# Mixture-of-experts stage: six more experts in fp32, another order of experts, and an earlier read of the first expert's slots

## The chip, the cores and the metric

One core of a Trainium2 chip runs the whole layer as one launch. The metric is the device time of one execution in microseconds (us); lower is better. TensorE is called PE in the profile, VectorE DVE, ScalarE ACT, GpSimd POOL, SyncE SP. PE's weight loads are listed apart as PEld.

## What is computed

The layer is an attention mixer (neighbourhood attention and grouped-query attention over 1024 tokens and a context of 256) followed by a mixture of 32 experts, of which each token takes 4. The change touches the experts alone. Cut to what matters:

```python
logits = h @ w_router + b_router
top_logits, top_e = lax.top_k(logits, 4)
top_w = softmax(top_logits)
# for each expert e, the tokens xe that chose it:
gu = xe @ w_gu[e] + b_gu[e]                  # 1024 -> 2048
x_glu = minimum(gu[:, :1024], 7.0)
x_lin = clip(gu[:, 1024:], -7.0, 7.0)
act = (x_lin + 1) * (x_glu * sigmoid(1.702 * x_glu))
yb = act @ w_dn[e] + b_dn[e]                 # 1024 -> 1024
y[token] += yb * top_w                       # summed over the 4 experts of a token
x = x + gt2 * rmsnorm(y, g_post_ffn)
```

All data is fp32, and the result must be close to fp32.

## The kernel before

The program runs its phases one after another: modulation and projections, attention, output projections with the router, then the experts (`Moe2.moe`, line 1441), a loop for tokens over the capacities (`overflow`, which has no rounds here), and the last norm (`final`, line 1411).

**Ranks and capacities.** The router's code counts the tokens of each expert and ranks the experts by count. Rank r has room for `CAPS[r]` tokens (line 2056): ranks 0 to 15 for 304 down to 136, ranks 16 to 24 for 128, ranks 25 to 31 for 96 down to 56. The program is fixed for the ranks; which expert has a rank is read from `erow` into a register (`ereg`), and the weight DMAs use it as an address. For each of its ranks the table of slots in DRAM (`slots_d`) lists token number and weight; the router's code writes it by indirect DMAs of POOL, and the last of these end just before the experts begin.

**Three forms of an expert** (`mode`, line 1466). A weight piece is 128 x 1024 fp32 (512 KB); a step works on four pieces, and an expert has six steps: four U steps (of `w_gu`) and two D steps (of `w_dn`), 24 pieces.
- "T", over 128 tokens: the weights are stationary. Each piece is split into two parts, hi (ACT, `split_hi`, line 1523) and lo (DVE, `split_lo`, line 1532), which PE takes in its faster reduced fp32 form; the tokens are split in the same way and stand beside each other, so that a matmul of hi goes over 2c columns and one of lo over 256 (`tra`, lines 1692 to 1697).
- "N", 128 tokens: split as well, with the tokens stationary and 512 columns of weights moving, three matmuls for each (`nat`, lines 1659 to 1668).
- "F", up to 96 tokens: plain fp32, no split. The weights are stationary in halves of 64 columns, two halves side by side (`few`, line 1717). In the trace each of these matmuls shows as two rows, 128 rows a step.

**Order of steps.** `positions()` gives each place p = 0 to 31 a rank: even places take the wide experts from rank 0 (304 tokens) on, odd places first the seven F experts from rank 31 (56) on, then the nine N experts. `steps` (line 1480) weaves the pair p, p + 1: U of p + 1 and U or D of p in turn, with the next pair's first two U steps in between the D steps. In the very last pair no next pair is there, so its two D steps of p + 1 stand behind each other; in the very first, the two U steps of place 0 do.

**Buffers and queues.** SP issues all weight DMAs. Split pieces go to `raw5` (6 buffers), and from there to `hi5` (6) and `lo5` (5); F pieces go to `rawf` (4 buffers, one step). A piece of F is loaded into the buffer that a matmul step has just left (`load_whole`, line 1720, in the second pass of `few`). When the last F expert is done, the space of `rawf` becomes two more buffers each of `hi5` and `lo5`. Splits and loads for the split experts are issued from `slot` (line 1592), called after each piece of a T or N step. `slot` also moves the chains of work behind a step (activation, next split) and takes one item off the queues `hot` and `cold`: transposes of an N expert's activations, of the next expert's gathered tokens (`xtr`), and of results (`one` in `step_D`, line 1861). A call from an F step moves the chains only and leaves these queues alone.

**Results.** `scatter` (line 1879) adds a tile of results to the sums in DRAM (`f_d`) by an indirect DMA of POOL, each behind the one before, as they write the same tensor. `final` reads `f_d` when all have landed.

**Start.** Before, SP loads six pieces of place 0 (line 1903), ACT and DVE split four, and the slots of places 0 and 1 are read from ACT's queue behind the third split (line 1915); `gather(0)` then fetches the tokens and `prepare(0)` transposes them.

## Time and profile before

| | us |
|---|---|
| median of 3 runs | 2760.55 |
| lowest, highest | 2759.66, 2763.95 |
| the profiled execution | 2763.18 |
| its span in the profile | 2761.6 |
| PE busy in the span | 2627.6 (95%) |
| DVE, ACT, POOL busy | 1754.1, 1419.0, 560.7 |

The span is the time from the first to the last instruction of the profiled execution. Its experts run from some 1150 us (first weights asked for) to some 2727 us (sums read). A row of the timeline gives the start, the duration, engine and line, what is written and read, and in brackets how long the engine had been idle and what released it. Matmuls overlap, so the time from one start to the next is what one costs. SPq, ACTq stand for the queue's part: the issue of DMAs.

### The profile page before, as it was taken

The page shows a single profiled execution, that of the slowest core. Times are in us where ns is not written, and L with a number is a line of the kernel's source. Part 1 is how long each engine was busy: PE and PEld are TensorE (multiplying, and loading weights), DVE is VectorE, ACT ScalarE, POOL GpSimd, SP SyncE. Part 2 cuts the span into 40 slices and gives each one's busy share as a digit, 9 for nine tenths or more (in the row PEclk, how much of TensorE's full clock was granted, in tenths as well). Part 3 has the DMA queues.
Part 4 walks back from the last instruction along what each step waited for, and adds up shares of the span by engine and source line. Part 5 has one row for each costly group of instructions (what it writes and reads, how often), then busy time and mean ns, then how long its engine had stood idle before and what let it go on. Part 6 is the DMA issues. An engine that isn't in the chain of part 4 may idle for free. (4 is left out here: it accounts for less than half of the span.)

```text
span 2761.6 us, 52451 instructions
## 1 busy us (share of the span) xinstructions
PE 2627.6 (95%) x19986; PEld 2246.1 (81%) x19986; DVE 1754.1 (64%) x3001; ACT 1419.0 (51%) x2334; POOL 560.7 (20%) x485
## 2 busy tenths in 40 slices
PE   6999999999999999599999999999999999999993
PEld 3788887555588778499999999999999999899892
DVE  3722332667688546554555655566888888888895
ACT  3422111555577424434444445446777777777773
POOL 2310001556644232400110011001101100111001
PEclk9999999999999999799999999999999999999996
DMA  6224561501233243566788898888889988998896
GB/s 240 73 95 162 196 197 60 171 16 33 43 76 74 106 145 132 167 225 222 276 287 272 291 298 287 287 294 286 278 281 309 301 286 299 314 309 293 299 312 227
DMA packets 197423, 588.16 MB, mean 213 GB/s; under 512 B 50400, under 2 KB 57136, under 8 KB 197024
## 3 DMA queue, kind: packets, MB, share of 16 engines
q1 hardware_dynamic: 174432, 521.51, 55.1%
q0 software_dynamic: 19152, 61.86, 8.4%
q8 instruction: 158, 2.59, 0.4%
q10 hardware_dynamic: 3584, 1.40, 0.3%
q14 instruction: 97, 0.79, 0.1%
HBM read 527.92 MB, written 58.08 MB: 212 GB/s over the span
## 5 line engine op out<-in xcount | busy, mean ns | idle before, releaser
L1532 DVE TENSOR_TENSOR lo<-raw,hi 128x1024 fp32r<-128x1024 f32 x600 | 719.5, 1222 | 347.8 <-ACT hi L1523 219.0
L1523 ACT ACTIVATE hi<-raw 128x1024 fp32r<-128x1024 f32 x600 | 626.4, 1054 | 130.5 <-PE g L1692 59.7
L1692 PE MATMUL g<-xT,hi 128*128 128x320 f32 (+10 forms) x1792 | 522.1, 333 | 0.0
L1693 PE MATMUL g<-xT,lo 128*128 128x256 f32 x1792 | 484.2, 281 | 0.0
L1692 PEld LDWEIGHTS g<-xT,hi 128*128 128x128 f32 x1792 | 337.2, 188 | 12.3 <-issue 0.3
L1693 PEld LDWEIGHTS g<-xT,lo 128*128 128x128 f32 x1792 | 337.6, 188 | 1.5
L1881 POOL DMA_INDIRECT f_d<-y,slot x34 | 62.5, 1838 | 1206.0 <-ACT y L1869 1062.7
L1692 PE MATMUL g<-aT,hi 128*128 128x288 f32 (+10 forms) x896 | 262.9, 335 | 0.0
L1693 PE MATMUL g<-aT,lo 128*128 128x256 f32 x896 | 241.8, 280 | 0.0
L174 DVE TENSOR_TENSOR wlo<-raw,whi 128x1024 fp32r<-128x1024 f32 x33 | 42.1, 1290 | 218.5 <-ACT whi L173 218.3
L1692 PEld LDWEIGHTS g<-aT,hi 128*128 128x128 f32 x896 | 168.5, 188 | 5.8
L1693 PEld LDWEIGHTS g<-aT,lo 128*128 128x128 f32 x896 | 168.9, 188 | 0.4
L859 ACT ACTIVATE p<-S 128x512 f32<-128x512 f32 x160 | 94.2, 596 | 103.7 <-PE S L858 99.0
L613 DVE TENSOR_REDUCE mn<-S 128x1 f32<-128x512 f32 x180 | 100.9, 595 | 66.4 <-PE S L612 66.0
L1717 PE MATMUL g<-xN,rawf 128*64 128x88 f32 (+5 forms) x3584 | 131.5, 234 | 1.8 <-issue 0.8
L1717 PEld LDWEIGHTS g<-xN,rawf 128*64 128x64 f32 x3584 | 125.9, 137 | 7.7 <-issue 5.6
L400 PE MATMUL mm<-hTh,whi 128*128 128x512 f32 (+1 forms) x416 | 123.9, 385 | 1.7 <-ACT whi L173 1.7
L400 PE MATMUL mm<-hTh,wlo 128*128 128x512 f32 (+1 forms) x416 | 123.2, 384 | 0.0
L400 PE MATMUL mm<-hTl,whi 128*128 128x512 f32 (+1 forms) x416 | 123.1, 383 | 0.0
L1666 PE MATMUL g<-hi,xN 128*128 128x512 f32 x288 | 117.6, 408 | 0.0
L1668 PE MATMUL g<-lo,xN 128*128 128x512 f32 x288 | 113.7, 395 | 0.0
L1667 PE MATMUL g<-hi,xN 128*128 128x512 f32 x288 | 113.6, 395 | 0.0
(416 smaller groups left out, 5727.3 us busy)
## 6 DMA issues: line engine op xcount, KB each, us to landing
raw<-in_w_gu_dram SPq DMA_DIRECT2D x400, 512.0 KB
raw<-in_w_dn_dram SPq DMA_DIRECT2D x200, 512.0 KB
rawf<-in_w_gu_dram SPq DMA_DIRECT2D x112, 512.0 KB
rawf<-in_w_dn_dram SPq DMA_DIRECT2D x56, 512.0 KB
raw<-in_w_mod_dram SPq DMA_DIRECT2D x40, 512.0 KB
raw<-in_w_in_dram SPq DMA_DIRECT2D x34, 512.0 KB
x<-in_x_dram SPq DMA_DIRECT2D x16, 512.0 KB
sig_d<-stg POOLq DMA_DIRECT2D x16, 512.0 KB
```

The lines of the kernel that those rows point to most:

```text
L400: T.matmul(ps[:, :n], w[:, ks], h[:, k, a:a + n], start=k == 0 and pi == 0, stop=k == KT - 1 and pi == 2)
L613: nc.vector.tensor_reduce(out=u.mn[:, i, j:j + 1], in_=ps[:, :n], op=ALU.min, axis=AX.X)
L859: nc.scalar.activation(u.p[t // 2][:, t % 2 * 512:t % 2 * 512 + 512], ps, AF.Exp, scale=-1.0)
L1523: ACT.activation(hi, raws[i], AF.Copy)
L1532: V.tensor_tensor(out=lo, in0=raws.pop(i), in1=f(his[split[i]]), op=ALU.subtract)
L1666: T.matmul(ps[:m], x[:, kk, P:P + m], hi[:, cs], start=False, stop=False)
L1667: T.matmul(ps[:m], x[:, kk, :m], hi[:, cs], start=False, stop=False)
L1668: T.matmul(ps[:m], x[:, kk, :m], lo[:, cs], start=False, stop=kk == 7)
L1692: T.matmul(ps[:, :2 * c], hi[:, cs], x[:, kk, :], start=first, stop=False)
L1693: T.matmul(ps[:, :256], lo[:, cs], x[:, kk, :256], start=False, stop=last)
L1717: T.matmul(ps[a:a + 64, i, r * 256:r * 256 + c], w[:, cs:cs + 64], x[:, kk, :], start=kk == 0, stop=kk == 7)
L1881: G.indirect_dma_start(out=self.f_d, out_offset=bass.IndirectOffsetOnAxis(ap=SL[p][xi][:n, 0:1], axis=0), in_=Y[p][xi][:n], in_offset=None ...
```

## The change

Three things. Experts of 136 to 160 tokens (ranks 10 to 15) take the form "F" too; `few` gets a second layout of its results for them (two PSUM tiles, one pass over the weights, a load behind each piece), while the old one, now called `tight`, stays for the small experts beside a "T" expert. The order of places goes from rank 15 through 10 to 9 down to 0 on the even places, beside the nine N experts first and then the F experts of 96 down to 56. And the slots of place 0 are read on SP in front of all weights. The two extra buffers of `hi5` and `lo5` go away, since F experts now last to the end. Whether a place has its data in the wide tiles is now asked by `wide_of(p)`, p even.

```diff
-            mode.append("T" if c > P else "N" if c > CF else "F")
+            mode.append("F" if c <= CF or P < c <= 160 else "T" if c > P else "N")
+        wide_of = lambda p: p % 2 == 0
...
-            n = N_HI + 2 if "hi5" in more else N_HI - 1
             for _ in range(2):
-                if st["h"] - st["c"] < n:
+                if st["h"] - st["c"] < N_HI - 1:
                     split_hi()
-                if st["s"] - st["c"] < n - 1 + ("hi5" not in more):
+                if st["s"] - st["c"] < N_LO:
                     split_lo()
...
         def few(key, x, p, evac):
             c = caps[posr[p]]
-            ps = gps.tile([P, 2, 512], F32, name="g5")
-            for r in range(2):
+            tight = mode[p - 1] == "T" and not wide_of(p)
+            ps = [gps.tile([P, 2, 512], F32, name="g5") for _ in range(1 if tight else 2)]
+            out = ps if not tight else [ps[0][:, h].rearrange("p (i c) -> p i c", i=2) for h in range(2)]
+            for r in range(2 if tight else 1):
                 for q in range(4):
                     wants(key, q)
                     w = his[key + (q,)]
                     for k in range(2):
                         kk = q * 2 + k
-                        for i in range(2):
+                        for i in (r, 2 + r) if tight else range(4):
                             for a in (0, 64):
-                                cs = k * 512 + (i * 2 + r) * P + a
-                                T.matmul(ps[a:a + 64, i, r * 256:r * 256 + c], w[:, cs:cs + 64], x[:, kk, :],
+                                cs = k * 512 + i * P + a
+                                T.matmul(out[i // 2][a:a + 64, i % 2, :c], w[:, cs:cs + 64], x[:, kk, :],
                                          start=kk == 0, stop=kk == 7)
-                    if r:
+                    if r or not tight:
                         load_whole()
-                    if q % 2 and r + q < 4:
+                    if q < 3 if not tight else q % 2 and r + q < 4:
                         slot(p)
...
-        load(N_RAW)
+        slots(0)
+        load_whole(N_F)
+        slots(1)
         columns(0)
         columns(1)
+        load(N_RAW)
+        gather(0)
...
-        for i in range(4):
-            split_hi()
-            split_lo()
-            load()
-            if i == 2:
-                slots(0, "scalar")
-                gather(0)
-                slots(1, "scalar")
-                G.memset(f(bhl[64:P]), 0.0)
+        G.memset(f(bhl[64:P]), 0.0)
         prepare(0)
         while cold or chains:
             advance()
-        split_hi(N_HI - 4)
-        split_lo(N_LO - 4)
-        load(2)
-        load_whole(N_F)
+        split_hi(4)
+        split_lo(4)
+        load(4)
...
-    wide, rest = list(range(N_WIDE)), list(range(31, 24, -1)) + list(range(N_WIDE, 25))
+    few, mid = list(range(25, 32)), list(range(16, 25))
     o = []
-    while wide or rest:
-        if wide:
-            o.append(wide.pop(0))
-        if rest:
-            o.append(rest.pop(0))
+    for r in [15, 14, 13, 12, 11, 10] + list(range(N_T - 1, -1, -1)):
+        o += [r, mid.pop(0) if mid else few.pop(0)]
     return o
```

Three places show the new order of instructions; the number behind a name is its buffer.

SP at the start of the experts, before: `h2_d` is the last store of the router's phase, `erow` the expert numbers, `raw5` split pieces of place 0, `bcol` biases, `slot_10174` the slots of place 2 (those of places 0 and 1 are on ACT's queue).

```order
L1018 DMA h2_d_90<-h2_9874 128x1024
L1475 TENSOR_LOAD erow_10006
...
L1496 DMA raw5_10081<-in_w_gu_dram 128x1024
...
L1496 DMA raw5_10091<-in_w_gu_dram 128x1024
...
L1555 DMA bcol_10093<-in_b_col_dram 128x24
...
L1548 DMA slot_10174<-slots_d_103 128x3x2
```

The same place now: `rawf` pieces are those of place 0, `raw5` those of place 1.

```order
L1018 DMA h2_d_90<-h2_9874 128x1024
L1475 TENSOR_LOAD erow_10006
...
L1542 DMA slot_10081<-slots_d_103 128x2x2
...
L1496 DMA rawf_10083<-in_w_gu_dram 128x1024
...
L1496 DMA rawf_10089<-in_w_gu_dram 128x1024
...
L1496 DMA raw5_10104<-in_w_gu_dram 128x1024
...
L1496 DMA raw5_10189<-in_w_gu_dram 128x1024
...
L1496 DMA rawf_10210<-in_w_gu_dram 128x1024
```

The slots of place 0 moved in front of the weights; the pieces of place 0's second step (`rawf_10210` on) stand behind ten pieces of place 1.

PE at the end of the experts, before: `yT` are results of place 30 waiting for their transpose, `aN` the activations of place 31, `nov` the first instruction behind the experts.

```order
L1868 MATMUL t5_28742<-ident_60,yT_28713 128x128 x4
...
L1868 MATMUL t5_28757<-ident_60,yT_28713 8x128 x4
...
L1668 MATMUL g5_28734<-lo5_28657,aN_28068 128x512
L1659 MATMUL g5_28777<-bhl_10041,oneh_27792 128x512
...
L1354 TENSOR_LOAD nov_10018
```

The same place now: the two D steps of place 31 (56 tokens, results in `g5_27854` and `g5_27932`).

```order
L1714 MATMUL g5_27854<-aN_27007,rawf_27686 64x56 x8
...
L1714 MATMUL g5_27932<-aN_27007,rawf_27895 64x56 x8
...
L1714 MATMUL g5_27932<-aN_27007,rawf_27925 64x56 x8
L1865 MATMUL t5_28002<-ident_60,yT_27836 128x128 x4
L1865 MATMUL t5_28009<-ident_60,yT_27836 128x128 x4
L1865 MATMUL t5_28016<-ident_60,yT_27836 48x128 x4
L1865 MATMUL t5_28023<-ident_60,gx_27927 56x128 x4
L1865 MATMUL t5_28029<-ident_60,gx_27997 56x128 x4
L1354 TENSOR_LOAD nov_10018
```

The transposes of results stood among the last steps' matmuls; five groups of them now stand behind the last.

POOL at the end, before: the two tiles of place 30 (136 tokens) and the one of place 31 (128), added to `f_d`.

```order
L1881 DMA f_d_104<-y5n_27725,slot_25659 1152x1024
L1881 DMA f_d_104<-y5_28578,slot_26288 1152x1024
L1881 DMA f_d_104<-y5_28597,slot_26288 1152x1024
L1881 DMA f_d_104<-y5n_28733,slot_26736 1152x1024
L1354 TENSOR_LOAD nov_10018
```

The same place now: three tiles of place 30 (304 tokens) and one of place 31 (56).

```order
L1878 DMA f_d_104<-y5n_26538,slot_23968 1152x1024
L1878 DMA f_d_104<-y5_27753,slot_24693 1152x1024
L1878 DMA f_d_104<-y5_27786,slot_24693 1152x1024
L1878 DMA f_d_104<-y5_27817,slot_24693 1152x1024
L1878 DMA f_d_104<-y5n_27853,slot_25212 1152x1024
L1354 TENSOR_LOAD nov_10018
```

The last pair has one tile more to add than before.

## Rows read from the trace of the kernel before

**Rows 1.** Busy time by stretch: from and to, length, then busy us and instructions of PE, PEld, DVE, ACT and POOL, PE's granted clock as a share of full speed, busy share of the DMA engines, GB/s.

```profile
1320.00:1340.00 20.00, 19.84 (x268) 19.17 (x268) 13.46 (x24) 8.29 (x11) 2.43 (x2) 1.00 0.95 319
...
2300.00:2600.00 300.00, 297.75 (x1934) 269.76 (x1933) 263.26 (x362) 222.69 (x333) 31.68 (x21) 1.00 0.88 302
```

**Rows 2.** What PE waited for from 1290 to 2720 us, the two longest: who waited, for whom, us in total, times, longest.

```profile
PE t L1746 <- DVE gx L1740: 4.2, 5, 1.5
PE t L1626 <- DVE xT L1613: 1.6, 7, 0.3
```

**Rows 3.** Timeline of PE (start us, us, what): the first and the next step's first row of a fp32 step of 72 tokens and of one of 96, with the matmuls around the second.

```profile
1441.37 0.41 PE L1717 MATMUL g<-xN,rawf 128*64 128x72 f32 x6
...
1445.52 0.50 PE L1692 MATMUL g<-xT,hi 128*128 128x512 f32 x1
...
1825.12 0.34 PE L1692 MATMUL g<-xT,hi 128*128 128x400 f32 x1
1825.30 0.28 PE L1693 MATMUL g<-xT,lo 128*128 128x256 f32 x1
1825.50 0.47 PE L1717 MATMUL g<-xN,rawf 128*64 128x96 f32 x6
...
1830.93 0.45 PE L1692 MATMUL g<-xT,hi 128*128 128x400 f32 x1
1831.22 0.28 PE L1693 MATMUL g<-xT,lo 128*128 128x256 f32 x1
```

**Rows 4.** Timeline of PE: the first row of a split step of 160 tokens and of the 128-token step behind it, and the same of a split step of 136 tokens.

```profile
2182.74 0.31 PE L1692 MATMUL g<-xT,hi 128*128 128x320 f32 x1
...
2191.22 0.40 PE L1659 MATMUL g<-bhl,oneh 128*128 128x512 f32 x1
...
2637.06 0.29 PE L1692 MATMUL g<-xT,hi 128*128 128x272 f32 x1
...
2644.91 0.39 PE L1659 MATMUL g<-bhl,oneh 128*128 128x512 f32 x1
```

**Rows 5.** Timelines of SP, POOL, ACT, PE and DVE at the start of the experts, put in order of time.

```profile
1150.94 6.53 SPq L1496 DMA_DIRECT2D raw<-in_w_gu_dram  x6
...
1153.53 1.85 POOL L1293 DMA_INDIRECT slots_d<-data,sl  x1 [0.23 <-issue]
...
1156.14 1.06 ACT L1523 ACTIVATE hi<-raw 128x1024 fp32r<-128x1024 f32 x1 [0.96 <-DMA raw<-in_w_gu_dram]
...
1160.69 1.59 ACTq L1548 DMA_DIRECT2D slot<-slots_d  x2
...
1167.34 1.00 POOL L1564 DMA_INDIRECT xg<-h_d,slot  x1 [11.97 <-DMA slot<-slots_d]
...
1172.04 1.09 PE L1626 MATMUL t<-ident,xg 128*128 128x128 f32 x4 [19.88 <-DMA xg<-h_d,slot]
1173.16 0.60 ACT L1610 ACTIVATE xT<-t 128x512 fp32r<-128x512 f32 x1 [9.77 <-PE t L1626]
1173.79 0.69 DVE L1613 TENSOR_TENSOR xT<-t,xT 128x512 fp32r<-128x512 f32 x1 [9.14 <-ACT xT L1610]
...
1179.97 0.62 PE L1695 MATMUL g<-xT,hi 128*128 128x304 f32 x1
...
1185.20 0.46 PE L1697 MATMUL g<-xT,lo 128*128 128x304 f32 x1
1185.46 0.39 PE L1695 MATMUL g<-xT,hi 128*128 128x304 f32 x1
...
1186.66 0.30 PE L1697 MATMUL g<-xT,lo 128*128 128x304 f32 x1
1186.80 0.30 PE L1695 MATMUL g<-xT,hi 128*128 128x304 f32 x1
```

**Rows 6.** Busy time by stretch (columns as in rows 1) at the end of routing.

```profile
1120.00:1140.00 20.00, 16.21 (x96) 14.23 (x94) 13.58 (x45) 12.08 (x28) 8.97 (x16) 0.86 0.36 132
1140.00:1160.00 20.00, 6.47 (x38) 5.38 (x38) 12.57 (x46) 5.75 (x8) 9.26 (x15) 0.50 0.63 145
```

**Rows 7.** Timeline of POOL: scatters of results of a 280-token expert (its first tile of 128 rows was issued at 1400.12) and those of the last pair.

```profile
1409.18 1.60 POOL L1881 DMA_INDIRECT f_d<-y,slot  x1 [7.47 <-DMA f_d<-y,slot]
1416.23 1.38 POOL L1881 DMA_INDIRECT f_d<-y,slot  x1 [5.45 <-DMA f_d<-y,slot]
...
2705.32 2.39 POOL L1881 DMA_INDIRECT f_d<-y,slot  x1 [64.96 <-ACT y L1869]
2716.41 1.35 POOL L1881 DMA_INDIRECT f_d<-y,slot  x1 [8.71 <-ACTq L1355]
2720.24 1.57 POOL L1881 DMA_INDIRECT f_d<-y5n,slot  x1 [2.48 <-issue]
```

**Rows 8.** Timelines of PE, ACT and SP at the end of the experts, put in order of time: a transpose of results and its copy, the read of the x tiles, the last matmul, the read of the sums.

```profile
2689.01 0.60 PE L1868 MATMUL t<-ident,yT 128*128 128x128 f32 x4
...
2689.65 0.69 ACT L1869 ACTIVATE y<-t,slot 128x512 f32<-128x512 f32 x1 [0.48 <-PE t L1868]
...
2697.50 9.52 SPq L1951 DMA_DIRECT2D raw<-x_d  x6
...
2714.37 0.39 PE L1668 MATMUL g<-lo,aN 128*128 128x512 f32 x1
...
2727.17 2.50 SPq L1421 DMA_DIRECT2D lo<-f_d  x5
```

More of the change, by code (lines that the diff above doesn't have):

```diff
@@ L1507, in load_whole @@
                 if st["f"] < len(whole):
-                    his[whole[st["f"]]] = fetch(more["f"], "rawf", whole[st["f"]])
+                    his[whole[st["f"]]] = fetch(rfp, "rawf", whole[st["f"]])
                     st["f"] += 1
-        def part(pool, name, i):
-            if name in more and i % 4 == 3:
-                pool = more[name]
-            return pool.tile([P, 1024], F32R, name=name)
         def split_hi(n=1):
@@ L1521, in split_hi @@
                     return
-                his[split[i]] = hi = part(hip, "hi5", i)
+                his[split[i]] = hi = hip.tile([P, 1024], F32R, name="hi5")
                 ACT.activation(hi, raws[i], AF.Copy)
@@ L1530, in split_lo @@
                     return
-                los[split[i]] = lo = part(lop, "lo5", i)
+                los[split[i]] = lo = lop.tile([P, 1024], F32R, name="lo5")
                 V.tensor_tensor(out=lo, in0=raws.pop(i), in1=f(his[split[i]]), op=ALU.subtract)
@@ L1569, in xalloc @@
             c = caps[posr[p]]
-            if mode[p] == "T":
-                return xtp.tile([P, 8, 2 * CT], F32R, name=name + "T")[:, :, :2 * c], c
+            if wide_of(p):
+                m = xtp.tile([P, 8, 2 * CT], F32R, name=name + "T")
+                return (m[:, :, :2 * c], c) if mode[p] == "T" else (f(m)[:, :, :c], None)
             m = xtp.tile([P, 8, 2 * P], F32R, name=name + "N")
@@ L1815, in step_D @@
             if j == 0:
-                Y[p] = [wk.tile([P, D], F32, name="y5n")] if mode[p] != "T" else {}
+                Y[p] = {} if wide_of(p) else [wk.tile([P, D], F32, name="y5n")]
             if mode[p] == "N":
@@ L1834, in step_D @@
             got, yts = [], []
-            room = "yT" if mode[p] == "T" else ("yF", j)
+            room = "yT" if wide_of(p) else ("yF", j)
             def ev(h, ps):
@@ L1840, in ev @@
                     todo[room] = len(tiles(p))
-                    yts.append(wk.tile([P, 4, CT], F32, name="yT") if mode[p] == "T" else
+                    yts.append(wk.tile([P, 4, CT], F32, name="yT") if wide_of(p) else
                                wk.tile([P, 2, CT], F32, name="gx", bufs=4).rearrange("p a b -> p (a b)")[:, :4 * CF]
@@ L1861, in one @@
             def one(xi, a, n):
-                if j == 0 and mode[p] == "T":
+                if j == 0 and wide_of(p):
                     Y[p][xi] = wk.tile([P, D], F32, name="y5", bufs=3)
@@ L1936, in moe @@
                 los.pop((k, p, j, q), None)
-            if (k, p, j) == whole[-1][:3]:
-                fctx.close()
-                more.clear()
-                more.update({n: self.pool(self.early, n + "b", 2, side="right") for n in ("hi5", "lo5")})
         while hot or cold or chains:
```

7 lines of the change are left out of this document (4 added, 3 removed).

## Prediction

> **What bounds the kernel now.** I read the busy time by stretch first. From 2300 to 2600 us TensorE is busy 298 of 300 us at the full clock, DVE 263, and the DMA engines are 88% busy [rows 1]. Then the waits: over the whole expert stage TensorE's two longest waits sum to 5.8 us [rows 2]. So in the middle a step costs what its matmuls cost, and relief of DVE and ACT buys nothing by itself. The two places where TensorE stands still are the ends: between routing and the first expert (its first matmul is at 1179.97, [rows 5]) and after the last matmul at 2714.37 [rows 8].
>
> **The six experts in fp32.** A fp32 step of 72 tokens lasts from 1441.37 to 1445.52, 4.15 us, one of 96 from 1825.50 to 1830.93, 5.43 us [rows 3]. That is 0.0533 us per token. Continued to the new sizes: 8.84 us at 160 tokens, 8.42 at 152, 7.99 at 144, 7.56 at 136. No row shows a fp32 step over 96 tokens; the two rows give a straight line and I take it. A split step without any transposes in it lasts 2182.74 to 2191.22, 8.48 us, at 160 tokens, and 2637.06 to 2644.91, 7.85, at 136 [rows 4]; between them by the line 8.27 at 152 and 8.06 at 144. Summed over 160, 160, 152, 144, 144 and 136 tokens: 49.64 in fp32 against 49.20 split, times six steps: **+2.6 us**. The fp32 form wins at 136 and 144 and gives it back at 160. The 144 hi and 144 lo splits that go away had been on engines with slack, so I cost them at nothing.
>
> The matmul behind a fp32 step starts late: after the step that ends at 1830.93 the next one follows only at 1831.22, 0.29 us, where the same spacing is otherwise 0.18 (1825.12 to 1825.30) [rows 3]. The 128-token experts now stand behind fp32 steps 36 times: 36 x 0.11 = **+4.0 us**. The Trainium skill, TensorEngine Tiling (Array Packing), Tiling Modes, Key Properties, says that a change of tiling mode drains TensorE, and these steps use 64-column tiles between 128-column ones; it gives no price. That speaks against the change, and the trace agrees, with the 0.11 us.
>
> **The start.** Before, SP begins the first expert's weights at 1150.94; ACT issues the slot read only at 1160.69, behind its splits, and POOL gathers at 1167.34; the first transpose is at 1172.04, the first matmul at 1179.97 [rows 5]. Now SP's slot read stands in front of all weights, so everything on that queue waits for the last slot write, issued from 1153.53 for 1.85 us. The shortest scatter shows 3.83 us from its start to the next engine action (2716.41 to 2720.24, [rows 7]), so this one has landed at some 1157.7. The read itself was 6.65 us with weights in front (1160.69 to 1167.34); no row shows it alone. I take 3.5, the bounds being 2 and 6.65. Gather at 1161.2, then 4.7 us to the first transpose as before, then four groups of transposes in place of six, 4 us: first matmul at 1170. **-10.0 us** (bounds -7 to -11.5).
>
> But the first two steps are both of expert 0, and its four buffers hold one step. The second step's weights can't be asked for before the first step frees a buffer, and on SP they stand behind ten pieces of expert 1, the last four of which wait for splits. They are the 15th piece, after two pieces' worth of gathered rows. At 319 GB/s with the engines 95% busy [rows 1] a 512 KB piece takes 1.56 us at best; the first takes 5.2 from issue to use (1150.94 to 1156.14, [rows 5]). With SP free at 1158.3 the 17th lands at 1158.3 + 5.2 + 16 x 1.56 = 1188.5. The first step ends at 1180.3: 5.5 us at the low clock (as from 1179.97 to 1185.46, where spacings go from 0.26 to 0.14 us), which do 2.75 us of its 7.56, and 4.8 more. So TensorE waits **+8.2 us** (0 to 11). Between 1120 and 1160 the granted clock fell from 0.86 to 0.50 as TensorE went from 16 busy us in 20 to 6 [rows 6], that is to 1.2 GHz; the same 2.75 us is lost again: **+2.7** (0 to 2.75). By the Trainium skill, DMA: Bandwidth & Descriptors, Specifications, a core gets some 358 GB/s of HBM; an estimate by it makes a piece 1.46 us and the wait 6.6. The row gives the slower rate, and I keep it.
>
> Expert 1's transposes, which had slots in the first two steps before, now stand inside its own first step, so that step waits for transpose, ACT copy and DVE subtract (0.60, 0.60 and 0.69 us in [rows 5, 8], and hand-overs): **+2.2** (0 to 3). The start together: -10.0 + 8.2 + 2.7 + 2.2 = +3.1 us.
>
> **The end.** The last two steps are both of a 56-token expert. Its second step's four pieces are asked for as the first step's last 1.94 us free the buffers, one each 0.49 us, and nothing stands between the steps. At 5.2 us for the first piece and 1.56 for each more, the last lands 2.5 + 5.2 + 4.7 = 12.4 us after the first step's start; then 0.5 and the second pass of 1.94 us, or twice that if the clock falls: 15.5 where 7.8 is the clean time of the two. **+7.2** taken, 5 to 9.
>
> In these fp32 steps no token transposes are issued (a step of this mode skips that queue), so the second half of the 304-token expert's output, three tiles, is transposed after the last matmul, and four scatters follow that add to one tensor and go one after the other. Before, the way from the last matmul to the read of the sums was 2714.37 to 2727.17, 12.8 us [rows 8]. Now: 1.9 us to the first scatter (transpose 0.64, ACT 0.69, hand-overs, [rows 8]); 11.1 for 128 rows while the x tiles are read (2705.32 to 2716.41); 7.05 for the next 128 rows (1409.18 to 1416.23); then 48 rows and 56 rows, between 3.83 (8 rows) and 7.05 (128): 4.9 and 5.2 [rows 7]. Sum 30.1, so **+17.3** (11 with no traffic, 21 if the second is as slow as the first).
>
> **Sum.** +2.6 + 4.0 + 3.1 + 7.2 + 17.3 = +34.2 us. The profiled execution took 2763.18 us (span 2761.6), 2.6 over the median of 2760.55; on the median I predict 2760.55 + 34.2, 2795 us. The reversal of the pairs costs nothing itself, as each wide expert keeps its partner. The two hi and two lo buffers that came free late before never come now, which touches three pairs with wide experts, where DVE is near 88% busy; no wait on a split shows in the stage without them [rows 2], and I put it at 0 (0 to 6).
>
> **Rivals.**
> *The line breaks (faster).* Beyond 128 tokens a fp32 step costs less per token than the line, as the cost of a step isn't all columns. At half the slope above 96 tokens it would be 7.13 at 160 and 6.50 at 136; that saves 36 steps some 1.42 us each, 51 us, and gives 2744. It beats the kernel before when the steps average under 7.3 us. Against it: rows of 72 and 96 tokens have TensorE's column time and nothing else in their difference (24 columns x 128 rows in the trace at 2.4 GHz is 1.28 us).
> *The ends come cheap.* The second step's weights are in time (-10.9) and the scatters meet no traffic (-6): 2778. For it: the slot read is early; against: the queue order and the buffer count.
> *Weights come late throughout.* An fp32 expert has four pieces ahead where the split experts had up to fourteen. A pair of experts moves 48 pieces, 25.2 MB, and 2.4 MB of rows gathered and added, in some 92 us (five pairs from 2182.74 to 2637.06, 90.9 each, [rows 4], and 1.1 more): 300 GB/s, where 319 at 95% busy [rows 1] allow 336. If each fp32 step waits 1 us for its first piece, that is 36 us more, 2831. Against it: a buffer freed in one step is needed 11.5 to 12.5 us later, after the rest of that step and a 128-token step, and a piece takes 5.2.
> *The early slot read doesn't come early* is inside the forecast's bounds, since the gain there is spent anyway.
>
> **How the numbers follow.** Forecast 0.63; ends cheap 0.15; late weights 0.14; the line breaks 0.08. The forecast alone spans 2782 to 2808 by its bounds. The range for 8 in 10 takes in the cheap ends and part of the late weights: 2770 to 2820. A difference under 0.2% (5.5 us) can't be told from none. Faster: the line breaks, 0.07. Same: 0.06, from its weak form and from all bounds at their low end. Slower: 0.87.
>
> **What would show it.** Right: the first matmul at about 1170, an idle TensorE between expert 0's first and second step with fp32 weights as the releaser, fp32 steps of 8.8 us at 160 tokens, a wait before the last fp32 step, and four scatters after the last matmul with some 30 us to the read of the sums. Wrong: fp32 steps under 8 us at 160 tokens, or a read of the sums within 20 us of the last matmul; if TensorE has waits for fp32 weights in the pairs of 136 to 160 tokens, the third rival holds.

## The result, and the profile after

The changed kernel takes 2789.69 us (median of 4 runs, 2787.72 to 2794.57), the kernel before 2761.11 beside it: a ratio of 1.0105 (95% interval 1.0087 to 1.0122), 28.6 us slower. 2795 was predicted, with a range of 2770 to 2820.

The profiled execution has a span of 2786.9 us. Its phases ahead of the experts, which the change doesn't touch, ended 4.8 us sooner than in the profile of before: the last slot write starts at 1148.76, where it was 1153.53 [rows 5]. So I compare from that write on. To the end of the span it is 1638.2 us, where it was 1608.0: **+30.2 us** in the experts and the last norm. The table under the experiments cuts this into stretches for every kernel.

What TensorE waited for, from 1140 to 2750 us, the longest first (columns as in [rows 2]):

```profile
PE t L1620 <- DMA raw<-in_w_gu_dram: 15.8, 1, 15.8
PE g L1714 <- DMA rawf<-in_w_gu_dram: 8.7, 5, 6.1
PE g L1714 <- DMA rawf<-in_w_dn_dram: 4.9, 4, 2.5
PE t L1620 <- DVE xT L1607: 3.7, 3, 1.4
```

The first row is the gap between routing and the first transpose; it names a weight transfer, but by the times it is the gather on another queue that was awaited (issued at 1154.85, below). The next two are the forecast waits for fp32 weights, 6.1 of the 8.7 in one piece. No other wait of the middle comes to 4 us.

**The start.** Timelines of POOL, SP and PE, put in order of time; they answer to [rows 5]:

```profile
1148.76 1.78 POOL L1293 DMA_INDIRECT slots_d<-data,sl  x1 [0.22 <-issue]
1152.00 0.42 SPq L1542 DMA_DIRECT2D slot<-slots_d  x1
1152.64 1.93 SPq L1496 DMA_DIRECT2D rawf<-in_w_gu_dram  x4
1154.85 1.00 POOL L1558 DMA_INDIRECT xg<-h_d,slot  x1 [4.30 <-DMA slot<-slots_d]
...
1163.20 1.61 PE L1620 MATMUL t<-ident,xg 128*128 128x128 f32 x8 [15.81 <-DMA raw<-in_w_gu_dram]
...
1166.55 9.41 PE L1714 MATMUL g<-xT,rawf 128*64 128x136 f32 x128
1182.01 10.20 PE L1714 MATMUL g<-xT,rawf 128*64 128x136 f32 x128 [6.05 <-DMA rawf<-in_w_gu_dram]
1192.14 0.50 PE L1653 MATMUL g<-bhl,oneh 128*128 128x512 f32 x1
...
1200.57 7.63 PE L1714 MATMUL g<-xT,rawf 128*64 128x136 f32 x128
```

The slot read takes 2.85 us (1152.00 to 1154.85) where it took 6.65. The gather behind it takes 8.35 (1154.85 to 1163.20) where it took 4.7: the DMA engines were 98% busy at 359 GB/s beside it, where they had been 79% busy at 241 in the 4.7. The first step of expert 0 takes 9.4 us and the second 10.1, where the third takes 7.6: TensorE's clock is low twice, on both sides of the 6.05 us of waiting for the second step's weights. It was granted 0.74 of full speed over the 20 us from 1160, and 0.74 again over the 10 us from 1182:

(Busy time by stretch, columns as in [rows 1].)

```profile
1160.00:1180.00 20.00, 12.59 (x144) 11.59 (x144) 7.10 (x12) 6.93 (x10) 3.01 (x4) 0.74 1.00 382
1182.00:1192.00 10.00, 9.99 (x128) 9.94 (x128) 0.20 (x1) 0.00 (x0) 0.00 (x0) 0.74 0.62 191
```

In the first stretch the DMA engines are busy all the time, at 382 GB/s.

**A fp32 step of 160 tokens** and the 128-token step behind it, on PE (answers to [rows 3, 4]):

```profile
1547.37 0.39 PE L1661 MATMUL g<-hi,aN 128*128 128x512 f32 x1
1547.60 0.39 PE L1662 MATMUL g<-lo,aN 128*128 128x512 f32 x1
1547.92 8.91 PE L1714 MATMUL g<-xT,rawf 128*64 128x160 f32 x128
1556.76 0.50 PE L1653 MATMUL g<-bhl,oneh 128*128 128x512 f32 x1
1557.10 0.40 PE L1660 MATMUL g<-hi,xN 128*128 128x512 f32 x1
1557.33 0.39 PE L1661 MATMUL g<-hi,xN 128*128 128x512 f32 x1
```

The step lasts 8.84 us (1547.92 to 1556.76), as predicted to the hundredth; the other sizes read 8.42, 7.99 and 7.57 from the same timeline. The 128-token step pays on both sides: 0.34 us behind its first matmul (1556.76 to 1557.10) and 0.32 ahead of the fp32 step (1547.60 to 1547.92), where the spacing is otherwise 0.23. The start is late behind 30 of the 36 steps; behind the other six stand transposes.

**The end.** Timelines of PE, POOL and SP, in order of time (answers to [rows 7, 8]):

```profile
2709.78 3.95 PE L1714 MATMUL g<-aN,rawf 128*64 128x56 f32 x128
2716.22 0.93 PE L1714 MATMUL g<-aN,rawf 128*64 128x56 f32 x16 [2.49 <-DMA rawf<-in_w_dn_dram]
2719.27 1.11 PE L1714 MATMUL g<-aN,rawf 128*64 128x56 f32 x16 [2.13 <-DMA rawf<-in_w_dn_dram]
...
2726.26 1.29 PE L1865 MATMUL t<-ident,yT 128*128 128x128 f32 x8
...
2728.13 1.57 POOL L1878 DMA_INDIRECT f_d<-y,slot  x1 [87.03 <-ACT y L1866]
2735.16 1.56 POOL L1878 DMA_INDIRECT f_d<-y,slot  x1 [5.46 <-issue]
2741.95 1.39 POOL L1878 DMA_INDIRECT f_d<-y,slot  x1 [5.23 <-DMA f_d<-y,slot]
2746.84 1.47 POOL L1878 DMA_INDIRECT f_d<-y5n,slot  x1 [3.50 <-issue]
2752.35 2.51 SPq L1421 DMA_DIRECT2D lo<-f_d  x5
```

The two last fp32 steps take 16.5 us (2709.78 to 2726.26), where two steps at full clock are 7.8. Of the 8.7 us more, 4.9 are waits for weights; the rest goes with the clock, of which 0.50 was granted from 2721.8 to 2726.3. Then come the transposes, four scatters one behind the other (7.03, 6.79, 4.89 and 5.51 us) and the read of the sums, 26.3 us behind the last matmul where it was 12.8 [rows 8].

### The profile page after: what moved, and what is told of

Its sections match the earlier page's. It is cut to its first block, busy times and chain, and to the rows that moved or that the text cites. A ratio compares the mean times of both kernels' runs of the same rounds, so it can differ in the third digit from the quotient of the medians.

```text
span 2786.9 us, 56263 instructions
## 1 busy us (share of the span) xinstructions
PE 2634.0 (95%) x22290; PEld 2238.5 (80%) x22290; DVE 1558.8 (56%) x2809; ACT 1236.6 (44%) x2070; POOL 547.4 (20%) x485
## 5 line engine op out<-in xcount | busy, mean ns | idle before, releaser
L1526 DVE TENSOR_TENSOR lo<-raw,hi 128x1024 fp32r<-128x1024 f32 x456 | 553.3, 1223 | 427.5 <-ACT hi L1517 268.3
L1517 ACT ACTIVATE hi<-raw 128x1024 fp32r<-128x1024 f32 x456 | 470.9, 1052 | 47.8 <-PE g L1686 17.5
L1686 PE MATMUL g<-xT,hi 128*128 128x368 f32 (+6 forms) x1024 | 320.8, 355 | 0.0
L1687 PE MATMUL g<-xT,lo 128*128 128x256 f32 x1024 | 286.1, 280 | 0.0
L1714 PE MATMUL g<-xT,rawf 128*64 128x144 f32 (+3 forms) x3072 | 204.6, 295 | 7.3 <-DMA rawf<-in_w_gu_dram 7.3
L1714 PEld LDWEIGHTS g<-xT,rawf 128*64 128x64 f32 x3072 | 198.0, 139 | 15.7 <-issue 7.3
L1686 PEld LDWEIGHTS g<-xT,hi 128*128 128x128 f32 x1024 | 192.3, 188 | 11.1
L1687 PEld LDWEIGHTS g<-xT,lo 128*128 128x128 f32 x1024 | 192.6, 188 | 0.6
L1686 PE MATMUL g<-aT,hi 128*128 128x368 f32 (+6 forms) x512 | 162.8, 358 | 0.0
L1660 PE MATMUL g<-hi,xN 128*128 128x512 f32 x288 | 118.6, 412 | 1.3 <-DVE xN L1607 1.3
```

Of the source, the lines that this page charges most:

```text
L1517: ACT.activation(hi, raws[i], AF.Copy)
L1526: V.tensor_tensor(out=lo, in0=raws.pop(i), in1=f(his[split[i]]), op=ALU.subtract)
L1660: T.matmul(ps[:m], x[:, kk, P:P + m], hi[:, cs], start=False, stop=False)
L1686: T.matmul(ps[:, :2 * c], hi[:, cs], x[:, kk, :], start=first, stop=False)
L1687: T.matmul(ps[:, :256], lo[:, cs], x[:, kk, :256], start=False, stop=last)
L1714: T.matmul(out[i // 2][a:a + 64, i % 2, :c], w[:, cs:cs + 64], x[:, kk, :], start=kk == 0, stop=kk == 7)
```

## The experiments

Each ratio is to the kernel before, run beside it on the same chip. The stretches are read from each kernel's own profile: from the start of the last slot write to the first matmul of the experts, on to the last, on to the issue of the first read of the sums, and all from that slot write to the end of the span. Each kernel has one profile, and single steps of the small fp32 experts wait for weights differently in each: against their clean lengths (3.88 us at 56 tokens to 5.43 at 96) they lose 2.0 us in sum in the changed kernel (its last two steps left out), 4.6 in the one before, and up to 11.1 in the others that have them with 64 columns. So a few us in the third or the last column are not shown to be an edit's.

| kernel | ratio (95% interval) | slot write to first matmul | to last matmul | to read of sums | slot write to end |
|---|---|---|---|---|---|
| before | 1 | 26.4 | 1534.4 | 12.8 | 1608.0 |
| changed | 1.0105 (1.0087 to 1.0122) | 17.8 | 1559.5 | 26.3 | 1638.2 |
| order_alone | 1.0128 (1.0112 to 1.0144) | 24.0 | 1562.8 | 26.7 | 1648.8 |
| form_alone | 1.0030 (1.0018 to 1.0042) | 27.5 | 1544.5 | 13.2 | 1619.1 |
| slots_early | 0.9988 (0.9979 to 0.9996) | 22.5 | 1537.8 | 14.0 | 1608.6 |
| drain_between | 1.0078 (1.0063 to 1.0093) | 17.8 | 1561.3 | 21.7 | 1635.6 |
| no_more | 1.0058 (1.0043 to 1.0074) | 27.1 | 1546.3 | 13.8 | 1621.9 |
| full_tiles | 1.0060 (1.0044 to 1.0075) | 17.1 | 1548.6 | 27.2 | 1627.9 |
| late_raw5 | 1.0098 (1.0080 to 1.0116) | 17.9 | 1553.6 | 31.1 | 1637.6 |
| end_split | 1.0038 (1.0025 to 1.0051) | 18.1 | 1555.3 | 13.7 | 1621.3 |
| full_small | 1.0336 (1.0322 to 1.0351) | 27.2 | 1629.9 | 15.0 | 1706.0 |
| full_slots | 1.0338 (1.0324 to 1.0352) | 25.5 | 1629.9 | 14.1 | 1704.0 |
| full_form | 1.0329 (1.0313 to 1.0345) | 27.0 | 1625.4 | 13.0 | 1699.6 |
| mended | 0.9986 (0.9973 to 0.9998) | 17.9 | 1542.4 | 15.7 | 1610.2 |

### One part at a time

**order_alone**: the kernel before with the new `positions()`, nothing else.

```diff
-    wide, rest = list(range(N_WIDE)), list(range(31, 24, -1)) + list(range(N_WIDE, 25))
+    few, mid = list(range(25, 32)), list(range(16, 25))
     o = []
-    while wide or rest:
...
+    for r in [15, 14, 13, 12, 11, 10] + list(range(N_T - 1, -1, -1)):
+        o += [r, mid.pop(0) if mid else few.pop(0)]
...
```

> The new order of experts with the old forms and the old start (all experts over 128 tokens split, slots read behind the third split). Theory of the ends (the loss comes from where the order puts the 304- and 56-token experts: late weights of the last fp32 step, about 8.7 us, and results transposed and added after the last matmul, about 13.3): 8.7 + 13.3, less some 2 for two groups of transposes fewer ahead of the first matmul, +20, 2781 us. Theory of the form (the six fp32 experts cost the time along their way, the order nothing): within 3 us of the kernel before, 2758 to 2764.

It came out at 1.0128, 36 us slower; in the last column it is 10.6 us above the changed kernel, though the intervals of the two ratios overlap. The end is as expected: 26.7 us to the read of the sums, and its last two fp32 steps take 15.6. But the stretch between first and last matmul is 28.4 us longer, not 8.7. What TensorE waited for from 1290 to 2720 us, the longest first:

```profile
PE t L1626 <- DVE xT L1613: 8.9, 8, 1.4
PE t L1746 <- DVE gx L1740: 6.8, 12, 1.1
PE g L1717 <- issue: 3.2, 9, 0.4
```

The first two rows are waits for DVE, 15.7 us where the kernel before had 5.8 [rows 2]. They fall in the pairs of a wide split expert and a 128-token one. In the old order those pairs run after the last small fp32 expert, with the two extra hi5 and lo5 buffers; in the new order they run without. So neither theory held as stated, and a third cause stood in the order, which no_more tests.

**no_more**: the kernel before, in which the extra buffers are never opened.

```diff
-            if (k, p, j) == whole[-1][:3]:
-                fctx.close()
-                more.clear()
-                more.update({n: self.pool(self.early, n + "b", 2, side="right") for n in ("hi5", "lo5")})
...
         es.close()
+        fctx.close()
```

> The kernel before with one edit: the two extra hi5 and lo5 buffers are never opened (the space of rawf stays closed to the end). Theory of the lost buffers (nine pairs of a split wide expert and a 128-token expert need them; the new order with the old forms showed TensorE idle for 14 us of its first 500): some 1.5 us a pair, 9 x 1.5 = 13.5, 2774 us. Rival (the 14 us came of the order itself): no change, 2761. The prediction put the same loss at 0 to 6 for the three pairs that are left in the changed kernel.

1.0058, 16 us; 13.9 in the table's last column, of which 11.9 lie between first and last matmul. From 1290 to 2720 us it waited:

```profile
PE t L1626 <- DVE xT L1613: 8.7, 8, 1.2
PE t L1746 <- DVE gx L1740: 6.4, 11, 1.0
```

Nearly the same sums in the same two rows as in order_alone: these waits come of the lost buffers. DVE isn't full there (87% at most in stretches of 100 us from 1900 on), but in the code its subtracts for lo, which now wait for a buffer, stand ahead of what TensorE needs. That last link is an argument from the code and was not tried apart. In order_alone, these 14 us, the 7.9 of the last steps and the 13.9 of the end make 36 of the 40.8 us in the last column, and 2.4 were gained ahead of the first matmul; some 7 us stay, 4.0 of them in the small fp32 experts (8.6 us over their clean lengths, 4.6 before).

**form_alone**: the changed kernel in the old order and with the old start.

```diff
-    few, mid = list(range(25, 32)), list(range(16, 25))
...
+    wide, rest = list(range(N_WIDE)), list(range(31, 24, -1)) + list(range(N_WIDE, 25))
...
-        slots(0)
-        load_whole(N_F)
-        slots(1)
...
+        load(N_RAW)
...
```

> The six experts of 136 to 160 tokens in fp32, in the old order and with the old start. Theory of the ends: only the step lengths (+2.6) and the starts of matmuls behind and in front of a fp32 step (36 times 0.1 to 0.2, 4 to 7) are left, so 2768 to 2771 us. Theory of the form: most of the 28.6 us is here, 2780 to 2789.

1.0030, 8 us. Between first and last matmul it is 10.1 us longer: 2.6 for the steps and 6.5 for the starts around them (36 x 0.09 ahead, 30 x 0.11 behind) make 9.1. Its waits about cancel: those for DVE fall from 5.8 to 2.8 us, those for fp32 weights rise from 0.7 to 3.5. The theory of the form falls. Set beside order_alone this says more: in the old order the fp32 form adds 11.1 us (last column); in the new one, form and early slot read together take 10.6 off (1648.8 to 1638.2), 6.2 of it ahead of the first matmul. No run has the form without the early read in the new order. The form needs no splits, and in the new order it stands in six of the nine pairs that have lost their buffers.

**slots_early**: the kernel before with the early read of slots.

```diff
+        slots(0)
         load(N_RAW)
+        slots(1)
         columns(0)
         columns(1)
+        gather(0)
...
-            if i == 2:
-                slots(0, "scalar")
-                gather(0)
-                slots(1, "scalar")
...
```

> The kernel before with one edit: the slots of place 0 are read on the first queue in front of all weights, and the gather of its tokens is issued at once. In the changed kernel the way from the last slot write to the first matmul was 17.8 us where it was 26.4. With the wide first expert (six groups of transposes, not four): about 20, a gain of 6, 2755 us. Rival: the weights that now wait for the slot write come late by as much, and nothing is gained, 2761.

0.9988, 3 us, half of what was expected. Timelines of POOL and PE:

```profile
1152.50 1.97 POOL L1293 DMA_INDIRECT slots_d<-data,sl  x1 [0.22 <-issue]
1158.73 1.00 POOL L1564 DMA_INDIRECT xg<-h_d,slot  x1 [4.26 <-DMA slot<-slots_d]
...
1167.15 1.09 PE L1626 MATMUL t<-ident,xg 128*128 128x128 f32 x4 [16.00 <-DMA raw<-in_w_gu_dram]
```

The gather starts 6.2 us behind the last slot write, where it was 13.8 [rows 5], 7.6 sooner. But it takes 8.4 us beside the weights that it overtook, where it took 4.7: the first transpose comes 3.9 sooner. In this profile 3.4 are lost again between first and last matmul, but not at the start: the small fp32 experts' steps are 11.1 us over their clean lengths, where the kernel before had 4.6. Whether that is the edit's doing is not shown.

### The end

**drain_between**: the changed kernel with the queued transposes issued between the last two steps.

```diff
         for k, p, j in steps:
+            while (k, p, j) == ("D", NE - 1, 1) and (hot or cold or chains):
+                advance()
             (step_U if k == "U" else step_D)(p, j)
```

> The changed kernel with one edit: the transposes that are still queued are issued between the last two fp32 steps, where TensorE waits for weights, not after the last. Theory of the ends: the three tiles of the 304-token expert are added some 11 us sooner, the chain of four scatters then ends some 10 sooner, 2779 us. Rival (the scatters are held up by the weights and x tiles on the same queues, whenever they start): 2787 to 2790.

1.0078; the gain is 2.6 us by the last column and some 7 by the ratios, whose intervals overlap. Where the edit acts, from the start of the last but one fp32 step (2716.55) to the read of the sums, it is 37.7 us where the changed kernel has 42.6: 4.9 gained. The scatters on POOL:

```profile
2722.30 1.57 POOL L1878 DMA_INDIRECT f_d<-y,slot  x1 [74.76 <-ACT y L1866]
2733.07 1.56 POOL L1878 DMA_INDIRECT f_d<-y,slot  x1 [9.21 <-issue]
2743.79 1.39 POOL L1878 DMA_INDIRECT f_d<-y,slot  x1 [9.15 <-DMA f_d<-y,slot]
```

They start sooner, and the first two take 10.8 and 10.7 us where they took 7.0 and 6.8: they run beside the last step's weights and the x tiles (307 and 322 GB/s, where the changed kernel has 231 and 77). 7.7 of the 10 us go back so.

**late_raw5**: the changed kernel with the very last step's weights read early, into raw5 buffers.

```diff
-                if st["l"] < min(len(split), st["s"] + N_RAW):
-                    raws[st["l"]] = fetch(rawp, "raw5", split[st["l"]])
+                if st["l"] < min(len(split) + 4, st["s"] + N_RAW):
+                    if st["l"] < len(split):
+                        raws[st["l"]] = fetch(rawp, "raw5", split[st["l"]])
+                    else:
+                        x = whole[st["l"] - len(split) - 4]
+                        his[x] = fetch(rawp, "raw5", x)
...
```

> The changed kernel with one edit: the four pieces of the very last step go to raw5 buffers, which are free by then, and so are asked for before the step ahead of it ends. Theory of the ends: the last two fp32 steps take 7.8 us, not 16.5, and all behind them comes 8.7 sooner, ratio to the kernel before 1.0074. Rival (the chain of scatters is slowed by as much, as it now runs beside the read of x tiles): 1.0105.

1.0098 against 1.0105: nothing that can be told apart. The two last steps do take 7.6 us, but the end grows by 4.7. From the start of these steps to the read of the sums it is 38.5 us (42.6), so 4.1 of the 8.9 stay. The last column hides them, as one step of 88 tokens, which the edit doesn't touch, takes 9.33 us where the changed kernel has 5.82. POOL and SP:

```profile
2702.47 23.13 SPq L1946 DMA_DIRECT2D raw<-x_d  x6
...
2726.05 1.57 POOL L1882 DMA_INDIRECT f_d<-y,slot  x1 [78.18 <-ACT y L1870]
2737.63 1.56 POOL L1882 DMA_INDIRECT f_d<-y,slot  x1 [10.01 <-issue]
2744.64 1.39 POOL L1882 DMA_INDIRECT f_d<-y,slot  x1 [5.44 <-DMA f_d<-y,slot]
```

The x tiles wait for raw5 buffers until the last step has left them, so their transfer falls on the first scatter, which takes 11.6 us instead of 7.0. The rival holds for half of it: what ends last is a chain of transfers, and the step that ends sooner meets more of them. But it meets them because this edit gave the x tiles' buffers to the weights; a kernel with early weights and early x tiles was not run.

**end_split**: the changed kernel with three split experts and their 128-token partners at the end.

```diff
-    for r in [15, 14, 13, 12, 11, 10] + list(range(N_T - 1, -1, -1)):
-        o += [r, mid.pop(0) if mid else few.pop(0)]
+    for r in [15, 14, 13, 12, 11, 10] + list(range(N_T)):
+        o += [r, few.pop() if r < 7 else mid.pop(0)]
```

> The changed kernel with one edit: the order of the wide split experts is 304, 280, 256, 224, 216, 208, 200 (beside 56 to 96), then 184, 184, 176 beside the last three 128-token experts, so that a 176- and a 128-token expert end the stage. Theory of the ends: no late weights in front of the last step (-8.7) and the end as in the kernel before (-13.3), ratio 1.0026, 2768 us. Rival (the ends are a part of it only, the order costs elsewhere too): over 1.006.

1.0038: 18 us of the expected 22, and the end is 13.7 us, about as before. Between first and last matmul only 4.2 of the 8.7 us came back: the small fp32 experts are 7.5 us over their clean lengths where the changed kernel had 2.0. One step of 80 tokens alone took 9.57 us, not 4.58, with waits for weights.

### The switch between tiles

**full_tiles**: the changed kernel with 128 columns of weights in a matmul for the six experts.

```diff
-                            for a in (0, 64):
+                            for a, m in ((0, 64), (64, 64)) if tight else ((0, P),):
                                 cs = k * 512 + i * P + a
-                                T.matmul(out[i // 2][a:a + 64, i % 2, :c], w[:, cs:cs + 64], x[:, kk, :],
+                                T.matmul(out[i // 2][a:a + m, i % 2, :c], w[:, cs:cs + m], x[:, kk, :],
```

> The changed kernel with one edit: the six experts of 136 to 160 tokens take 128 columns of weights in a matmul, not two times 64, with the same results. Theory of the tile switch (the late starts between fp32 and 128-token steps come of the change from 128- to 64-column tiles): the 36 x 0.2 us go, steps are as long as before, ratio to the kernel before 1.008 (changed kernel: 1.0105). Rival 1 (the late starts come of the change of data type): as the changed kernel, 1.0105. Rival 2 (the fp32 weight load of 128 columns isn't covered by the matmul): fp32 steps longer, over 1.02.

1.0060, 12 us less by the ratios. PE at a step of 160 tokens:

```profile
1542.85 0.40 PE L1662 MATMUL g<-lo,aN 128*128 128x512 f32 x1
1543.08 8.86 PE L1714 MATMUL g<-xT,rawf 128*128 128x160 f32 x64
1551.66 0.50 PE L1653 MATMUL g<-bhl,oneh 128*128 128x512 f32 x1
1552.01 0.40 PE L1660 MATMUL g<-hi,xN 128*128 128x512 f32 x1
```

The step lasts 8.58 us (1543.08 to 1551.66) where it lasted 8.84, and the start ahead of it is no longer late (0.23, not 0.32). 36 x (0.26 + 0.09) = 12.6 us; between first and last matmul the profile has 10.9. The matmuls within the step are no faster: a row of 128 columns starts every 0.136 us, and so does a pair of 64-column rows before. The 0.26 lies at the step's ends, 0.05 behind its first pair and 0.21 behind its last (that pair starts 0.24 us ahead of the next matmul, the last row of 128 columns 0.03). But the 0.35 behind the first matmul of the 128-token step (1551.66 to 1552.01) stays. So the late start that the prediction had priced, 0.11 us, is not the tile switch, and what causes it stays open; the switch costs 0.35 a step, most of it hidden in the fp32 step's own length.

**full_small**: the kernel before with 128 columns for its own experts of 56 to 96 tokens; **full_slots** the same with slots read on POOL's queue; **full_form** form_alone with 128 columns everywhere.

```diff
-                            for a in (0, 64):
-                                cs = k * 512 + (i * 2 + r) * P + a
-                                T.matmul(ps[a:a + 64, i, r * 256:r * 256 + c], w[:, cs:cs + 64], x[:, kk, :],
+                            cs = k * 512 + (i * 2 + r) * P
+                            T.matmul(ps[:, i, r * 256:r * 256 + c], w[:, cs:cs + P], x[:, kk, :],
...
```

> The kernel before with one edit: its own fp32 experts (56 to 96 tokens, 42 steps beside split ones) take 128 columns of weights in a matmul, not two times 64. Theory of the tile switch (in the changed kernel this edit took 0.26 us from each fp32 step and 0.09 from the step ahead of it, 12.6 in all for 36 steps): 42 x 0.3 to 0.35 = 13 to 15 us, 2747 us, ratio 0.995, faster than both kernels. Rival (beside the wide split experts the weights' transfers bind, DMA engines 73 to 88% busy, and the time goes into waits for weights): 0.998 to 1.

> The kernel of full_small with a second edit: the slots of places 0 and 1 are read on GpSimd's own queue, straight behind the slot writes, and the gather behind them, so that no weight waits for them. The read on the first queue brought the first matmul 3.9 us forward and made the fp32 weights late by 3.4. Theory (it was the weights held back that cost the 3.4): first matmul some 4 us sooner than in full_small and nothing lost behind it, ratio 0.0015 below that of full_small. Rival (the gather is slowed by the weights beside it, and gives it all back): the same ratio as full_small.

> The six experts of 136 to 160 tokens in fp32 in the old order and with the old start (as in form_alone), with 128 columns of weights in every fp32 matmul. Theory of the tile switch: form_alone's +8 to 11 us less 36 x 0.35 = 12.6 and less 42 x 0.35 = 14.7, some -17, 2744 us, ratio 0.994, that is level with full_small: the fp32 form of these six is worth about nothing once the switch is paid for. Rival (the extra hi5 and lo5 buffers that this form does without matter more when its steps are shorter): 0.997 or over.

All three missed by far: 1.0336, 1.0338 and 1.0329, 91 to 94 us slower. PE in full_small at a step of 88 tokens:

```profile
1808.16 0.28 PE L1693 MATMUL g<-xT,lo 128*128 128x256 f32 x1
1808.28 7.27 PE L1716 MATMUL g<-xN,rawf 128*128 128x88 f32 x64
1815.34 0.43 PE L1692 MATMUL g<-xT,hi 128*128 128x416 f32 x1
```

The step lasts 7.06 us (1808.28 to 1815.34) where 88 tokens took 5.00, and it lasts 7.06 at 56 tokens too: 64 rows at 110 ns each, whatever streams through them. So the tokens don't set this floor; that the load of 128 columns of weights does is likely, but not shown apart. With two times 64 columns the floor is 3.88 (56 and 64 tokens). By an estimate from these steps two times 64 is right below some 127 tokens (the line of 0.0533 us a token reaches 7.06 there) and one times 128 above; no size between 96 and 136 was run. Where the slots are read made no difference (1.0336 and 1.0338).

**mended**: the changed kernel with four edits: end_split's order; 128 columns for the six experts only; the extra buffers opened behind the last fp32 expert; expert 0's second step read into raw5 buffers at the start.

```diff
-                            for a in (0, 64):
+                            for a, m in ((0, 64), (64, 64)) if tight else ((0, P),):
...
+            if (k, p, j) == whole[-1][:3]:
+                fctx.close()
+                more.clear()
+                more.update({n: self.pool(self.early, n + "b", 2, side="right") for n in ("hi5", "lo5")})
...
-        load(N_RAW)
+        load(2)
+        for x in second:
+            his[x] = fetch(rawp, "raw5", x)
...
```

> The changed kernel with four edits that the runs so far price: the order of end_split (-18), 128 columns in a matmul for the six experts of 136 to 160 tokens only (-12; the experts up to 96 tokens keep two times 64), the two extra hi5 and lo5 buffers opened behind the last fp32 expert, for the three pairs left (-4), and the weights of place 0's second step read into raw5 buffers with the first ten pieces, so that TensorE doesn't wait 6 us for them (-8 with the clock). Theory (the four prices add): the changed kernel's 28.6 less 42, some 10 us under the kernel before, ratio 0.9955 to 0.998, faster than both. Rival (edits share their gain, as late_raw5 showed, where a step that ended sooner only waited at the next chain): 1.0 or over.

0.9986, 33 us under the changed kernel and some 4 under the one before. It beats the changed kernel clearly. Against the one before it is level: the ratio is 4 us under, its own profile 2.2 us over (last column). The result lies between the two expectations; of the 42 us that the prices sum to, 28 to 33 came. PE at the start, then the busy time of a stretch (columns as in [rows 1]):

```profile
1168.37 9.75 PE L1721 MATMUL g<-xT,rawf 128*128 128x136 f32 x64
1177.96 7.63 PE L1721 MATMUL g<-xT,raw 128*128 128x136 f32 x64
...
1190.43 0.80 PE L1667 MATMUL g<-hi,xN 128*128 128x512 f32 x1 [3.72 <-DVE xN L1614]
```

```profile
1190.40:1196.40 6.00, 5.97 (x14) 4.73 (x15) 3.32 (x4) 1.88 (x2) 0.00 (x0) 0.50 0.90 300
```

The wait for the second step is gone (6.05 to 0), and the second step is no longer slow (7.4 us to the next, not 10.1). But a wait of 3.72 us for DVE, behind late splits of expert 1, takes its place, and behind that wait the clock is granted 0.50 for 6 us: the slow stretch has moved with the wait. And the small fp32 experts are 10.4 us over their clean lengths, 6.5 of it in one step of 80 tokens, the one that was late in end_split too; what makes it late in this order was not tried.

## Why the prediction was right, and where its steps were off

The sign, the size and the places were right. Term by term:

| term | predicted | measured |
|---|---|---|
| fp32 in place of split steps | +2.6 | +2.6 (8.84, 8.42, 7.99, 7.57) |
| starts around fp32 steps | +4.0 | +6.5 (30 x 0.11 + 36 x 0.09) |
| first matmul sooner | -10.0 | -8.7 (26.4 to 17.8 behind the last slot write) |
| expert 0's second step, clock, expert 1's transposes | +13.1 | +8.5 to +9.4 |
| last fp32 step | +7.2 | +8.7 (16.5 less 7.8) |
| last matmul to read of sums | +17.3 | +13.5 |
| sum | +34.2 | +31.1 to +32.0; the whole stretch +30.2 |

The fourth row: the first two steps took 25.59 us (1166.55 to 1192.14) where two of the third's length are 15.14, so +10.5; the kernel before had lost 3.5 at the same place (30.8 for two steps of 13.67, 1179.97 to 1210.78), so +7.0; and expert 1's first step took 8.44 where the same step took 6.95 in the next pair and 6.03 in three later ones, +1.5 to +2.4.

That the sum came so near is luck in part: two terms were some 4 us too high each, three others 1 to 3 too low, and the small fp32 experts, which had no term, lost 2.6 us less than before. In its working the prediction has two slips. For the last fp32 step, 15.5 less 7.8 is 7.7, not the 7.2 that it took. And 2782 to 2808 isn't what its bounds give: all of them low make 2772, all high 2813.

**The six experts.** The straight line held beyond 96 tokens, so the rival "the line breaks" is out. form_alone bears out the first two rows (9.1 of its 10.1 us). What failed inside them is the cause given to the 0.11 us, which full_tiles keeps with 128-column tiles, and the late start ahead of the step, 0.09 us, which had no term. The Trainium skill's sentence (TensorEngine Tiling (Array Packing), Tiling Modes, Key Properties) that a change of tiling mode drains TensorE is borne out by the same run, at 0.35 us a step. I had not seen it because the line through the 72- and 96-token steps already contained 0.26 of it.

**The start.** The mechanism held: the slots come early, and expert 0's second step waits. The wait was 6.05 us, not 8.2: counted from the last slot write, the weights were there 1.7 us sooner than forecast, and the first step ended 0.4 later. They came at 382 GB/s and not at the 319 of [rows 1]. The kernel before had shown the higher rate at this very place (columns as in [rows 1]), and the prediction didn't read it:

```profile
1160.50:1167.30 6.80, 0.00 (x0) 0.00 (x0) 2.74 (x3) 1.32 (x2) 0.00 (x0) 0.50 1.05 395
```

The Trainium skill's 358 GB/s (DMA: Bandwidth & Descriptors, Specifications) are under the measured 382 too, and the 6.6 us estimated by it were nearer than mine. Another page of the Trainium skill (HBM Reference, Specifications (TRN2)) says that a core streaming alone measures about 425; the trace fits that one better, with 382 over 20 us and 421 from 2721.8 to 2726.3. The gain of the early read was cut by the gather, 8.35 us for 4.7, which no term had; the slot read, the last slot write and the transposes were 2.2 us shorter than taken. slots_early shows the slower gather alone.

**The end.** Both terms are in the trace, and their sum stands: 22.2 us for the 24.5 forecast. The first scatter took 7.0 us and not 11.1, which is the whole shortfall of the second term. That each could be had back alone doesn't follow. late_raw5 took away the wait for the last weights and kept 4.1 us, as the x tiles, which it had put off, fell on the scatters. drain_between took away the late transposes and kept 4.9 of the 10 expected, as its scatters ran beside the weights. Only end_split, which removes the whole arrangement, gave 17 to 18.

**The lost buffers.** They were put at 0 (0 to 6). In the changed kernel TensorE's waits for DVE in the three pairs left are 3.7 us, inside the bounds. But no_more shows that they are worth 1.3 to 1.5 us a pair, 12 to 14 in nine pairs, so the argument ("no wait on a split shows in the stage without them") was wrong: the stage that I had read ran beside fp32 experts, which need no splits.

**The rivals.** "The ends come cheap": the scatters did meet less traffic (7.0 and not 11.1 for the first), but the second step's weights were late; half of it came true. "Weights late throughout": waits for fp32 weights sum to 13.6 us, of which 6.1 lie in expert 0 and 4.9 in the last step; not throughout.

## What to carry to other kernels

Ask of a new order what each place in it had had for free: here the end of the old order hid a scatter chain, and its middle opened buffers that were worth 12 to 14 us. A wait at the very end is not sure to be a gain of its own while a chain of transfers stands behind it; take the wait away in an experiment before counting it. A form that costs 11 us in one order need cost nothing in another, so form and order have to be tried apart and together.

## What the runs showed of the hardware

- Matmuls of 64 columns between such of 128 cost 0.35 us for each fp32 step: 0.09 ahead of it and 0.26 in its length (8.84 to 8.58 us at 160 tokens).
- TensorE's granted clock was at the lower of its two levels, 1.2 GHz, behind waits: 0.50 for 6 us behind one of 3.72 us in mended, and 0.50 from 2721.8 to 2726.3 in the changed kernel's last fp32 step, behind two of 2.49 and 2.13.
- A fp32 matmul with 128 columns of weights has a floor of 110 ns a row (7.06 us for 64 rows at 56 to 96 tokens); two times 64 columns do the same work in 3.88 us at 56 and 64 tokens.
- A gather took 4.7 us in the kernel before (DMA engines 79% busy) and 8.4 us where it had overtaken the weights (98% and more); the first scatter of 128 rows at the end took 7.0 us in the changed kernel, 10.8 beside the last weights and 11.6 beside the x tiles.
- The DMA engines moved 382 GB/s over 20 us at the start of the changed kernel's experts, and 395 over 6.8 us in the kernel before, where a stretch in its middle shows 319 at 95% busy [rows 1].
